# Gated delta rule: the products of a triangular inverse over the whole TensorE array with the 64 changed columns, and norms from one-column products

## The chip, the cores and the metric

The kernel runs on one core of one Trainium2 chip. The metric is the device time of one execution in microseconds; smaller is better. One profiled execution gives the rows that are shown below.

## The reference

Two transformer-like blocks work on a sequence of 1024 tokens of width 1024, in float32. The change touches only the gated delta rule, one of the mixers of the first block: four heads of 128, computed in chunks. For each chunk and head a unit lower triangular system is solved, and q and k are normalised beforehand:

```python
def l2norm(x):
    return x * lax.rsqrt(jnp.sum(x * x, axis=-1, keepdims=True) + EPS)

def gated_delta_rule_chunked(q, k, v, g, beta):
    ...
    L = jnp.where(strict, jnp.einsum('nbhid,nbhjd->nbhij', kb, kc) * decay, 0.0)
    rhs = jnp.concatenate([vc * bc[..., None], kb * jnp.exp(gc)[..., None]], axis=-1)
    sol = lax.linalg.triangular_solve(eye + L, rhs, left_side=True, lower=True, unit_diagonal=True)
    u = sol[..., :Dv]
    w = sol[..., Dv:]
    ...
    def step(S, inp):
        v_new = u_i - jnp.einsum('bhcd,bhde->bhce', w_i, S)
        ...
```

Around it stand a conformer convolution (31 taps along time, `cfm_dw_w`), projections, an output projection, then cross attention, a feed-forward layer, and a second block of two further linear-attention mixers. None of these is changed.

## The kernel before, in words

All of the work is put on the engines in an order that a scheduler fixes when the program is built; each engine then goes through its own queue in that order and waits where data is not there.

The first stage works on two halves of 512 tokens. Dense projections are done by `mm3` (lines 178 to 180): three matmuls with 128 weight columns and 512 (or 256, 264) moving columns each, because weights and inputs are split into a high and a low part. The gated delta rule is the generator `gdn`, called four times: for the halves 0 and 1 and for the head pairs 0 and 1. `weave` runs it against a second generator with dense work (projections, the convolution of the conformer in `s1_conv`, its norm, the output projection), so that steps of both alternate. The calls take place at about 87 to 204, 237 to 364, 355 to 499 and 507 to 621 us of the profiled execution.

One call of `gdn` first sums the squares of q and k over d (lines 538 to 546): ACT squares four tiles of 128 x 512, each goes as the moving operand through a product with a block of 32 columns of ones (L541), the four results lie in four groups of 32 partitions, ACT copies them (L543), and four transposes (L546) turn them so that the token is the partition.

Then four chunks of 128 tokens follow, two chains of two, staggered by `LAG` steps. Each chunk inverts a 128 x 128 triangle per head (two heads together), made of two diagonal halves of 64 (`lo`, `hi`) and the block between them. Inside the halves it doubles the size of the inverted blocks in five levels. A level does the product `U` by `Xm` (L611), a copy to `Q` on ACT (L614), the product `Y` by `Q` (L617), two predicated copies on DVE into `Xm`, one for each half (L620), two transposes of `Xm` (L623) and a copy to `Y` on ACT (L625). Each product is done as four matmuls of 64 x 64 weights and 64 moving columns: two heads by two halves, each half in its own quadrant of the array. After the levels two more products give the block between the halves (L629, L634), with two matmuls of 64 x 64 each.

A float32 matmul stands in the trace as two records, and so does its weight load; a product of four matmuls is therefore `x8`.

DVE, besides the small steps of `gdn`, does the 31 taps of the conformer convolution (L480, 240 instructions of 128 x 512), which the scheduler is told to put at low priority; they lie between the predicated copies. POOL and ACT split the weights that come from HBM.

Of the kernel before, what the change touches and what calls it, by code (L numbers as in the profile page):

```python
# [9 lines left out]
F32 = mybir.dt.float32  # L10
F32R = mybir.dt.float32r
I32 = mybir.dt.int32
U8 = mybir.dt.uint8
AF = mybir.ActivationFunctionType
ALU = mybir.AluOpType
AX = mybir.AxisListType

P = 128
T = 1024
# [42 lines left out]
def weave(main, f, rate):  # L62
    """`rate` steps of f after each of main, then the rest of f"""
    due = 0.0
    for _ in main:
        due += rate
        while due >= 1:
            due -= 1
            next(f, None)
    run(f)  # L70


class Net:
# [72 lines left out]
    # weights: src [pairs of k tiles, 128, 2, columns]  # L146
# [14 lines left out]
    def wplan(self, specs):  # L161
        """the units that wpair() hands out, in order"""
# [3 lines left out]
    def wpair(self):  # L166
        """the next two k tiles, with the loads and splits of the following pairs under way"""
# [14 lines left out]
    # out[c, t]: 4 column tiles of 128, free = t  # L182
# [9 lines left out]
    # out[t, c]: t tiles of 128, free = columns  # L192
# [23 lines left out]
    # rows r [128, 1024] at t tile -> x hi/lo  # L216
# [12 lines left out]
    # rms norm of rows, times g, to x hi/lo  # L229
# [49 lines left out]
    def postnorm(self, y, g, hsrc, hdst):  # L279
        """y: two tiles [P, 4, 512]; y = hsrc + rms(y) g, also to hdst"""  # L280
# [12 lines left out]
    def norm_T(self, y, g, shift=None):  # L293
        """rms-normed rows of y (two panels), transposed"""
# [34 lines left out]
    def s1_open(self):  # L329
# [7 lines left out]
        lf = self.R([P, 6, P])  # L337
        nc.sync.dma_start(lf, a["lvl"])
        self.lvl = p.tile([P, 6, P], U8, name="lvl")
# [12 lines left out]
        nc.vector.tensor_scalar(self.nea, self.nea, -1.0, None, ALU.mult)  # L352
        self.S = []
# [5 lines left out]
    def s1_qkv(self, u, xh, xl, qk, vv, gate):  # L359
        """q, k, v of the heads 2u, 2u + 1 after the short convolution, [d, t], and their gates, rows"""  # L360
# [22 lines left out]
        # the heads 0 and 1 bring the eight logits along  # L383
# [31 lines left out]
    def s1_specs(self):  # L415
        """the weights of stage 1 in the order of their use"""
# [5 lines left out]
    def s1_ab(self, ab):  # L422
        """log decay and beta, [t, chunk, head]"""
# [37 lines left out]
    def s1_conv(self, j, xh, xl, cc):  # L461
        """gated and convolved conformer channels, [c, t]"""
# [52 lines left out]
    def gdn(self, u, qkv, dec, gate):  # L515
        """heads 2u, 2u + 1, 4 chunks of 128; multiplies the normed rows into `gate`"""
# [19 lines left out]
        # squares of q and k, summed over d  # L536
        pr = self.M()
        for j in range(4):
            sq = p1.tile([P, HT], F32, name="cv", tag="cv", bufs=2)
            nc.scalar.activation(sq, qk[:, j, :], AF.Square)  # L540
            mm(pr[32 * j : 32 * j + 32, :], lhsT=self.ones[:, 0:32], rhs=sq, start=True, stop=True)  # L541
        sq = p1.tile([P, HT], F32, name="cv", tag="cv", bufs=2)
        nc.scalar.copy(sq, pr)  # L543
        pn = self.M([P, 4, 4, 32])
        for c in range(NTT):
            tr(pn[:, c, :, :], sq[:, c * P : (c + 1) * P], self.ident)  # L546
        sk, qn, kn, bb, be, so = (p1.tile([P, 8], F32, name="gn", tag="gn", bufs=10) for _ in range(6))
        v.tensor_scalar(c42(sk), pn[:, :, 2:4, 0], EPS, None, ALU.add)
        v.tensor_scalar(c42(qn), pn[:, :, 0:2, 0], EPS, 128.0 * EPS, ALU.add, ALU.mult)
# [5 lines left out]
        def chunk(c):  # L555
# [19 lines left out]
            # decays  # L575
# [10 lines left out]
            # scores  # L586
# [8 lines left out]
            # (I + L)^-1 by doubling; U = -L^T, Xm the inverse within blocks, Y its transpose  # L595
            lv = lambda b: self.lvl[:, b, :].unsqueeze(1).to_broadcast([P, 2, P])
            Y = tl("Y", 2)
            nc.gpsimd.tensor_copy(Y, self.ident.unsqueeze(1).to_broadcast([P, 2, P]))
            v.copy_predicated(Y, lv(0), U)
# [6 lines left out]
            lo, hi = slice(0, 64), slice(64, P)  # L606
            for b in range(1, 6):
                pm = self.M([P, 8, 64], ns)
                for j in range(2):
                    for r in (lo, hi):  # L610
                        mm(pm[r, j, :], lhsT=U[:, j, r], rhs=Xm[:, j, r], start=True, stop=True)  # L611
# [3 lines left out]
                for j in range(2):  # L615
                    for r in (lo, hi):
# [848 lines left out]
```

## Time and profile before

| | |
|---|---|
| time, median of 3 runs | 3004.94 us (3001.94 to 3011.28) |
| span of the profiled execution | 3007.8 us |
| PE busy | 2823.5 us (94%) |
| DVE busy | 1813.9 us (60%) |
| ACT busy | 1135.2 us (38%) |
| POOL busy | 1234.5 us (41%) |
| gated delta rule and what is woven with it | about 86 to 622 us of the span |

The span runs from the first to the last instruction of the profiled execution; no time of that execution outside the span is given. Matmul records overlap, since they are pipelined: a busy share of PE says whether anything was in the array, and the pace is read from the starts of successive records.

### The profile page before, as it was taken

The numbers are of one execution on the slowest core, as the hardware profiler recorded it, in microseconds if no ns is written. First come the engines' busy times: TensorE is split into PE (matmuls) and PEld (weight loads), VectorE is DVE, ScalarE is ACT, GpSimd is POOL, SyncE is SP. The second block draws the span as 40 slices with busy tenths as digits, with TensorE's granted clock in tenths as the row PEclk, the third lists the DMA queues.
The fourth block names the chain that finished last, engine by engine and source line by source line (L and its number), as shares of the span: only waits on it lengthen the run. The fifth ranks groups of instructions, "written<-read, shape, count | busy, mean of one in ns | idle before, by whom it ended". The sixth has DMA issues, their size and how long they took to land.

```text
span 3007.8 us, 41965 instructions
## 1 busy us (share of the span) xinstructions
PE 2823.5 (94%) x15828; PEld 2232.1 (74%) x15828; DVE 1813.9 (60%) x3605; ACT 1135.2 (38%) x2273; POOL 1234.5 (41%) x913
## 2 busy tenths in 40 slices
PE   7999898998999999899899999999999999999998
PEld 6676676777877777677677777787777777777776
DVE  6698889866345765743855556737545366464444
ACT  4443534455444433233433333232233333232333
POOL 3333323333342554354454544343443543434443
PEclk9999999999999999999999999999999999999999
DMA  4112111146242633622422225121323332222222
GB/s 152 50 64 64 50 45 55 36 133 192 68 140 86 202 99 100 208 91 84 130 91 91 85 91 170 51 88 56 96 74 97 99 119 71 82 63 83 85 75 101
DMA packets 136715, 287.07 MB, mean 95 GB/s; under 512 B 9792, under 2 KB 12736, under 8 KB 136512
## 3 DMA queue, kind: packets, MB, share of 16 engines
q1 hardware_dynamic: 136512, 284.38, 29.3%
q8 instruction: 125, 2.05, 0.3%
q14 instruction: 78, 0.64, 0.1%
HBM read 265.99 MB, written 18.35 MB: 95 GB/s over the span
## 4 chain that ended last, share of the span: by engine, by line
PE 49%; DVE 14%; ACT 2%; issue 2%; DMA 2%; POOL 1%; SPq 0%; ACTq 0%; DVEq 0%; POOLq 0%
PE pa L178 15%; PE pa L179 14%; PE pa L180 14%; DVE fo L824 3%; PE pm L944 2%; DVE fo L822 1%; POOL wlo L144 1%; DMA wad<-in_w_ada 1%; DVE fo L829 1%; DVE fh L819 1%; DVE pad L818 1%; DVE gl L144 1%; PE pm L1001 0%; PE pm L990 0%; PE pm L1000 0%
## 5 line engine op out<-in xcount | busy, mean ns | idle before, releaser
L144 POOL TENSOR_TENSOR wlo<-raw,whi 128x512 fp32r<-128x512 f32 (+1 forms) x792 | 1137.7, 1442 | 1668.7 <-ACT whi L143 1590.6
L143 ACT CAST whi<-raw 128x512 fp32r<-128x512 f32 (+1 forms) x808 | 496.7, 620 | 1131.3 <-PE pa L180 603.8
L178 PE MATMUL pa<-x,whi 128*128 128x512 f32 x1376 | 567.4, 413 | 18.8 <-ACT x L1130 10.3
L178 PE MATMUL pa<-whi,x 128*128 128x512 f32 (+2 forms) x1408 | 555.3, 396 | 12.4 <-ACT z L1015 3.8
L180 PE MATMUL pa<-x,wlo 128*128 128x512 f32 x1376 | 552.1, 401 | 0.1
L179 PE MATMUL pa<-x,whi 128*128 128x512 f32 x1376 | 551.9, 401 | 0.0
L180 PE MATMUL pa<-whi,x 128*128 128x512 f32 (+2 forms) x1408 | 547.5, 389 | 0.0
L179 PE MATMUL pa<-wlo,x 128*128 128x512 f32 (+2 forms) x1408 | 546.4, 388 | 0.0
L178 PEld LDWEIGHTS pa<-x,whi 128*128 128x128 f32 x1376 | 261.7, 190 | 82.1 <-ACT x L1130 11.2
L178 PEld LDWEIGHTS pa<-whi,x 128*128 128x128 f32 x1408 | 265.5, 189 | 75.6 <-issue 6.3
L180 PEld LDWEIGHTS pa<-x,wlo 128*128 128x128 f32 x1376 | 261.7, 190 | 62.5 <-issue 2.7
L180 PEld LDWEIGHTS pa<-whi,x 128*128 128x128 f32 x1408 | 265.5, 189 | 54.0 <-issue 0.9
L179 PEld LDWEIGHTS pa<-wlo,x 128*128 128x128 f32 x1408 | 265.6, 189 | 52.4 <-issue 1.2
L179 PEld LDWEIGHTS pa<-x,whi 128*128 128x128 f32 x1376 | 262.1, 190 | 54.2 <-issue 3.4
L480 DVE SCALAR_TENSOR_TENSOR e<-padc,cw,e 128x512 f32<-128x512 f32 x240 | 197.3, 852 | 1.2
L824 DVE SCALAR_TENSOR_TENSOR fo<-pad,cols,fo 128x512 f32<-128x512 f32 x176 | 168.5, 985 | 0.7
L178 PE MATMUL pa<-whi,e 128*128 128x512 f32 x352 | 143.3, 407 | 25.8 <-DVE e L847 20.4
L819 DVE COPY fh<-pad 128x2 f32<-128x2 f32 x88 | 27.3, 310 | 196.4 <-ACT pad L817 196.4
L179 PE MATMUL pa<-wlo,e 128*128 128x512 f32 x352 | 142.2, 404 | 0.0
L180 PE MATMUL pa<-whi,gl 128*128 128x512 f32 x352 | 141.9, 403 | 0.0
L144 DVE TENSOR_TENSOR x<-pm,x 128x512 fp32r<-128x512 f32 x112 | 75.0, 685 | 67.8 <-ACT x L143 67.3
L178 PEld LDWEIGHTS pa<-whi,e 128*128 128x128 f32 x352 | 68.0, 193 | 46.7 <-DVE e L847 23.9
(354 smaller groups left out, 3848.7 us busy)
## 6 DMA issues: line engine op xcount, KB each, us to landing
raw<-in_w_in SPq DMA_DIRECT2D x112, 512.0 KB, 3.7
raw<-in_ffn_w_up SPq DMA_DIRECT2D x88, 512.0 KB, 3.8
raw<-in_ffn_w_down SPq DMA_DIRECT2D x44, 512.0 KB, 4.0
raw<-in_w_out SPq DMA_DIRECT2D x32, 512.0 KB, 3.9
raw<-in_w_qf SPq DMA_DIRECT2D x32, 512.0 KB, 3.7
h<-e SPq DMA_DIRECT2D x48, 256.0 KB, 3.0
r<-h SPq DMA_DIRECT2D x24, 512.0 KB, 4.5
wad<-in_w_ada SPq DMA_DIRECT2D x24, 512.0 KB, 4.4
```

The source lines that it names most:

```text
L143: self.nc.scalar.copy(hi, src)
L144: (lo_eng or self.nc.vector).tensor_tensor(lo, src, hi.bitcast(F32), ALU.subtract)
L178: mm(ps, lhsT=lh, rhs=rh, start=first, stop=False)
L179: mm(ps, lhsT=lh, rhs=rl, start=False, stop=False)
L180: mm(ps, lhsT=ll, rhs=rh, start=False, stop=last)
L480: v.scalar_tensor_tensor(o, pad[:, k : k + HT], w(k), o, ALU.mult, ALU.add)
L818: v.tensor_copy(pad[:, :2], fh[:, i, :])
L819: v.tensor_copy(fh[:, i, :], pad[:, HT:])
L822: v.tensor_scalar(o, pad[:, 2:], self.col(k0 + 2), self.col(FB0 + i), ALU.mult, ALU.add)
L824: v.scalar_tensor_tensor(o, pad[:, k : k + HT], self.col(k0 + k), o, ALU.mult, ALU.add)
L829: v.tensor_tensor(ua, ua, ub, ALU.mult)
L944: mm(pm[64 * e : 64 * e + 64, c, :], lhsT=kG[:, s], rhs=q[:, s], start=True, stop=True)
```

## The change

The two diagonal halves are no longer multiplied in quadrants. Since `U` and `Y` hold both halves in one 128 x 128 tile, one matmul per head over the whole array does both. A level changes only the columns of `Xm` whose bit of that level is 0, which are 64 of the 128, so these columns alone are the moving operand (`left`, a strided view), and one predicated copy over 128 partitions puts the result back; its mask is laid out for those 64 columns. The block between the halves is done over the whole array too, with a `Qz` whose other columns stay zero. For the norms, the squared tile becomes the weights, and one column of ones the moving operand: 16 products that give the sums with the token as the partition at once, so that the copy and the four transposes fall away.

```diff
-        lf = self.R([P, 6, P])
+        lf = self.R([P, P + 320])
...
+        self.Qz = []
+        for n in range(2):
+            z = p.tile([P, 2, P], F32, name=f"Qz{n}")
+            nc.gpsimd.memset(z, 0.0)
+            self.Qz.append(z)
...
-        pr = self.M()
+        pn = self.M([P, 4, 4])
         for j in range(4):
             sq = p1.tile([P, HT], F32, name="cv", tag="cv", bufs=2)
             nc.scalar.activation(sq, qk[:, j, :], AF.Square)
-            mm(pr[32 * j : 32 * j + 32, :], lhsT=self.ones[:, 0:32], rhs=sq, start=True, stop=True)
-        sq = p1.tile([P, HT], F32, name="cv", tag="cv", bufs=2)
-        nc.scalar.copy(sq, pr)
-        pn = self.M([P, 4, 4, 32])
-        for c in range(NTT):
-            tr(pn[:, c, :, :], sq[:, c * P : (c + 1) * P], self.ident)
+            for c in range(NTT):
+                mm(pn[:, c, j : j + 1], lhsT=sq[:, c * P : (c + 1) * P], rhs=self.ones[:, 0:1], start=True, stop=True)
...
             for b in range(1, 6):
-                pm = self.M([P, 8, 64], ns)
+                n, w = 64 >> b, 1 << b
+                left = Xm.rearrange("p h (n s w) -> p h n s w", s=2, w=w)[:, :, :, 0, :]
+                pm = self.M([P, 4, 64], ns)
                 for j in range(2):
-                    for r in (lo, hi):
-                        mm(pm[r, j, :], lhsT=U[:, j, r], rhs=Xm[:, j, r], start=True, stop=True)
+                    mm(pm[:, j, :], lhsT=U[:, j, :], rhs=left[:, j, :, :], start=True, stop=True)
                 yield
                 Q = tl("Q")[:, :, 0:64]
                 nc.scalar.copy(Q, pm[:, 0:2, :])
                 for j in range(2):
-                    for r in (lo, hi):
-                        mm(pm[r, 2 + j, :], lhsT=Y[:, j, r], rhs=Q[:, j, :], start=True, stop=True)
+                    mm(pm[:, 2 + j, :], lhsT=Y[:, j, :], rhs=Q[:, j, :], start=True, stop=True)
                 yield
-                for r in (lo, hi):
-                    v.copy_predicated(Xm[r, :, r], lv(b)[r, :, r], pm[r, 2:4, :])
+                mask = self.lvl[:, P + 64 * (b - 1) : P + 64 * b].rearrange("p (n w) -> p n w", w=w)
+                v.copy_predicated(left, mask.unsqueeze(1).to_broadcast([P, 2, n, w]),
+                                  pm[:, 2:4, :].rearrange("p h (n w) -> p h n w", w=w))
...
             pm = self.M([P, 4, 64], ns)
             for j in range(2):
-                mm(pm[hi, j, :], lhsT=U[lo, j, hi], rhs=Xm[lo, j, lo], start=True, stop=True)
+                mm(pm[:, j, :], lhsT=U[:, j, :], rhs=Xm[:, j, lo], start=True, stop=True)
             yield
-            Q = tl("Q")
-            nc.scalar.copy(Q[hi, :, lo], pm[hi, 0:2, :])
+            Q = self.Qz[ns]
+            nc.scalar.copy(Q[:, :, lo], pm[:, 0:2, :])
             for j in range(2):
-                mm(pm[lo, 2 + j, :], lhsT=Q[hi, j, lo], rhs=Y[hi, j, hi], start=True, stop=True)
+                mm(pm[:, 2 + j, :], lhsT=Q[:, j, :], rhs=Y[:, j, hi], start=True, stop=True)
```

The scheduler also moves instructions. In PE's queue the first levels of the first call of `gdn` stand as follows before; L178 to L180 are the dense matmuls, L602 and L623 transposes, L611 and L617 the two products of a level.

```order
L611 MATMUL pm<-Xm,U 64x64 x4
L602 MATMUL pm<-ident,Y 128x128 x2
L180 MATMUL pa<-x_126,wlo 128x512
L178 MATMUL pa<-x_126,whi 128x512
L617 MATMUL pm<-Q,Y 64x64 x4
L611 MATMUL pm<-Xm,U 64x64 x4
L179 MATMUL pa<-x_127,whi 128x512
L180 MATMUL pa<-x_126,wlo 128x512
L623 MATMUL pm<-ident,Xm 128x128 x2
L617 MATMUL pm<-Q,Y 64x64 x4
```

At the same place the changed program has (L613 and L618 are the products, L625 the transposes of `Xm`):

```order
L613 MATMUL pm<-Xm,U 128x64 x2
L179 MATMUL pa<-x_131,whi 128x512
L180 MATMUL pa<-x_130,wlo 128x512
L618 MATMUL pm<-Q,Y 128x64 x2
L602 MATMUL pm<-ident,Y 128x128 x2
L178 MATMUL pa<-x_130,whi 128x512
L625 MATMUL pm<-ident,Xm 128x128 x2
L179 MATMUL pa<-x_131,whi 128x512
L613 MATMUL pm<-Xm,U 128x64 x2
L180 MATMUL pa<-x_130,wlo 128x512
```

The products have half as many matmuls and still lie between dense matmuls; their places among these shift by one or two.

In PE's queue the norms of the first call read, before and then in the changed program (L541 and L547 are the products with ones, L546 the transposes):

```order
L541 MATMUL pm<-cv,ones 32x512
L180 MATMUL pa<-x_126,wlo 128x512
L178 MATMUL pa<-x_126,whi 128x512
L541 MATMUL pm<-cv,ones 32x512
L179 MATMUL pa<-x_127,whi 128x512
L180 MATMUL pa<-x_126,wlo 128x512
L178 MATMUL pa<-x_126,whi 128x512
L179 MATMUL pa<-x_127,whi 128x512
L546 MATMUL pm<-ident,cv 128x128 x4
```

```order
L547 MATMUL pm<-ones,cv 128x1 x8
L179 MATMUL pa<-x_131,whi 128x512
L180 MATMUL pa<-x_130,wlo 128x512
L178 MATMUL pa<-x_130,whi 128x512
L547 MATMUL pm<-ones,cv 128x1 x4
```

Eight or four one-column products now stand where one or two products of 512 columns stood, and nothing follows the last of them before DVE reads the sums.

In DVE's queue, late in the levels of the second call of `gdn`, the predicated copies (L620, now L621) stand between taps of the convolution (L480, now L485), before and then in the changed program:

```order
L620 COPY_PREDICATED Xm<-lvl,pm 64x2x64 x4
L480 SCALAR_TENSOR_TENSOR e_746<-padc,cw,e_746 128x512 x4
L620 COPY_PREDICATED Xm<-lvl,pm 64x2x64 x4
L480 SCALAR_TENSOR_TENSOR e_746<-padc,cw,e_746 128x512 x3
L620 COPY_PREDICATED Xm<-lvl,pm 64x2x64 x2
```

```order
L621 COPY_PREDICATED Xm<-lvl,pm 128x8x16
L485 SCALAR_TENSOR_TENSOR e_755<-padc,cw,e_755 128x512 x3
L621 COPY_PREDICATED Xm<-lvl,pm 128x8x16
L621 COPY_PREDICATED Xm<-lvl,pm 128x4x32
L485 SCALAR_TENSOR_TENSOR e_755<-padc,cw,e_755 128x512 x3
```

One copy of 128 partitions stands for two of 64, behind about as many taps as before.

## Rows read from the trace of the kernel before

**Rows 1.** The page: busy time by engine, then PE's clock in 40 slices.

```profile
PE 2823.5 (94%) x15828; PEld 2232.1 (74%) x15828; DVE 1813.9 (60%) x3605; ACT 1135.2 (38%) x2273; POOL 1234.5 (41%) x913
PEclk9999999999999999999999999999999999999999
```

**Rows 2.** Busy time by stretch, us: length, engines, clock, DMA share, GB/s.

```profile
86.00:400.00 314.00, 291.06 (x2139) 216.75 (x2140) 252.07 (x576) 141.63 (x330) 101.88 (x82) 0.99 0.17 55
400.00:580.00 180.00, 165.46 (x1161) 126.08 (x1160) 173.84 (x342) 76.65 (x185) 60.55 (x46) 0.97 0.16 50
580.00:622.00 42.00, 42.00 (x351) 31.68 (x352) 25.67 (x75) 24.88 (x68) 7.89 (x8) 1.00 0.09 26
```

**Rows 3.** Timeline, a lone level product between dense matmuls: start, duration, instruction.

```profile
306.94 0.40 PE L179 MATMUL pm<-x,whi 128*128 128x512 f32 x1
307.27 0.45 PE L617 MATMUL pm<-Q,Y 128*64 128x64 f32 x8
307.65 0.50 PE L180 MATMUL pm<-x,wlo 128*128 128x512 f32 x1
307.99 0.39 PE L178 MATMUL pm<-x,whi 128*128 128x512 f32 x1
308.21 0.40 PE L179 MATMUL pm<-x,whi 128*128 128x512 f32 x1
```

**Rows 4.** Timeline, two level products behind each other between dense matmuls.

```profile
314.31 0.28 PE L180 MATMUL pa<-whi,x 128*128 128x264 f32 x1
314.52 0.74 PE L611 MATMUL pm<-Xm,U 128*64 128x64 f32 x16
...
315.41 0.28 PE L179 MATMUL pa<-wlo,x 128*128 128x264 f32 x1
```

**Rows 5.** Timeline, a product for the block between the halves.

```profile
182.68 0.28 PE L180 MATMUL pa<-whi,x 128*128 128x256 f32 x1
182.89 0.44 PE L629 MATMUL pm<-Xm,U 64*64 64x64 f32 x4
...
183.49 0.28 PE L179 MATMUL pa<-wlo,x 128*128 128x256 f32 x1
```

**Rows 6.** Timeline, float32 matmuls over the whole array: 128, then 16 moving columns.

```profile
308.45 0.38 PE L589 MATMUL pm<-e 128*128 128x128 f32 x2
308.67 0.39 PE L590 MATMUL pm<-e 128*128 128x128 f32 x2
...
354.62 0.30 PEld L448 LDWEIGHTS pm<-glog,tri 128*128 128x128 f32 x2 [1.36 <-DVE glog L439]
354.83 0.30 PEld L449 LDWEIGHTS pm<-glog,ones 128*128 128x128 f32 x2
```

**Rows 7.** Groups of instructions, 86 to 640 us: count, busy us, mean ns, idle before.

```profile
L611 PE MATMUL pm<-Xm,U 128*64 128x64 f32 x640 | 36.5, 233 | 0.0
L620 DVE COPY_PREDICATED Xm<-lvl,pm 64x128 f32<-64x128 uint8 x160 | 47.7, 299 | 36.3 <-PE pm L617 15.6 <-ACT Y L625 9.7 <-ACT whi L143 4.1
L599 DVE COPY_PREDICATED Y<-lvl,U 128x256 f32<-128x256 uint8 x16 | 8.3, 519 | 0.0
```

**Rows 8.** Busy time of the predicated copies L620 alone, 400 to 580 us.

```profile
400.00:580.00 180.00, 12.48 (x42) 0.97 0.16 50
```

**Rows 9.** Timeline, one product with ones, then the four transposes of the norms.

```profile
238.32 0.40 PE L179 MATMUL pa<-x,whi 128*128 128x512 f32 x1
238.65 1.05 PE L541 MATMUL pm<-cv,ones 128*32 128x512 f32 x2
...
239.97 0.39 PE L178 MATMUL pa<-x,whi 128*128 128x512 f32 x1
...
242.31 0.60 PE L546 MATMUL pm<-ident,cv 128*128 128x128 f32 x4
```

**Rows 10.** Waits, 86 to 640 us: total, times, longest.

```profile
PE pm L623 <- DVE Xm L620: 6.2, 12, 1.3
PE pm L568 <- DVE Vs L574: 4.1, 3, 2.3
```

More of the change, by code (lines that the diff above doesn't have):

```diff
@@ L336, in s1_open @@
         self.trineg = ld("trineg", [P, P])
-        lf = self.R([P, 6, P])
+        lf = self.R([P, P + 320])
         nc.sync.dma_start(lf, a["lvl"])
-        self.lvl = p.tile([P, 6, P], U8, name="lvl")
+        self.lvl = p.tile([P, P + 320], U8, name="lvl")
         nc.gpsimd.tensor_copy(self.lvl, lf)
@@ L540, in gdn @@
             nc.scalar.activation(sq, qk[:, j, :], AF.Square)
-            mm(pr[32 * j : 32 * j + 32, :], lhsT=self.ones[:, 0:32], rhs=sq, start=True, stop=True)
-        sq = p1.tile([P, HT], F32, name="cv", tag="cv", bufs=2)
-        nc.scalar.copy(sq, pr)
-        pn = self.M([P, 4, 4, 32])
-        for c in range(NTT):
-            tr(pn[:, c, :, :], sq[:, c * P : (c + 1) * P], self.ident)
+            for c in range(NTT):
+                mm(pn[:, c, j : j + 1], lhsT=sq[:, c * P : (c + 1) * P], rhs=self.ones[:, 0:1], start=True, stop=True)
         sk, qn, kn, bb, be, so = (p1.tile([P, 8], F32, name="gn", tag="gn", bufs=10) for _ in range(6))
-        v.tensor_scalar(c42(sk), pn[:, :, 2:4, 0], EPS, None, ALU.add)
-        v.tensor_scalar(c42(qn), pn[:, :, 0:2, 0], EPS, 128.0 * EPS, ALU.add, ALU.mult)
+        v.tensor_scalar(c42(sk), pn[:, :, 2:4], EPS, None, ALU.add)
+        v.tensor_scalar(c42(qn), pn[:, :, 0:2], EPS, 128.0 * EPS, ALU.add, ALU.mult)
         ri = self.rsqrt(sk, 8, "g")
@@ L594, in chunk @@
             v.tensor_tensor(At, pk[:, 2:4, :], dd, ALU.mult)
-            lv = lambda b: self.lvl[:, b, :].unsqueeze(1).to_broadcast([P, 2, P])
             Y = tl("Y", 2)
             nc.gpsimd.tensor_copy(Y, self.ident.unsqueeze(1).to_broadcast([P, 2, P]))
-            v.copy_predicated(Y, lv(0), U)
+            v.copy_predicated(Y, self.lvl[:, 0:P].unsqueeze(1).to_broadcast([P, 2, P]), U)
             pm = self.M([P, 4, P], ns)
@@ L1431, in _host @@
                        & ((i[None, :] // b) % 2 == 1))
-    r["lvl"] = np.concatenate([lv[:, :1], lv[:, 1:6].transpose(2, 1, 0)], axis=1)
+    low = [lv[:, l].T.reshape(P, -1, 2, 1 << l)[:, :, 0, :].reshape(P, 64) for l in range(1, 6)]
+    r["lvl"] = np.concatenate([lv[:, 0]] + low, axis=1)
     r["hmask"] = np.tile(np.concatenate([lv[:64, :6, :64], np.eye(64, dtype=f)[:, None, :]], axis=1), (2, 1, 1))
```

## The prediction

> **What bounds the kernel now.** I first read the page [rows 1]: PE is busy for 94% of the span, no other engine for more than 60%, and the clock granted to PE is nine tenths or more of its upper level (2.4 GHz) in every slice. Then the busy times of the stretch in which the gated delta rule runs, cut into three [rows 2]. PE is busy there for 498.5 of 536 us (291.06 + 165.46 + 42.00), so 37.5 us are left in which nothing is in the array. DVE is the second to watch: 252 of 314 us before 400, but 173.84 of 180 between 400 and 580, which is 97%. So PE is the engine whose queue must get shorter, and in the middle stretch DVE's too.
>
> A busy share does not say what one product costs, so I read the timeline around single ones. Between dense matmuls of 512 columns, which follow each other every 0.23 us or a little less (307.99 to 308.21), a lone level product stands at 307.27 [rows 3]. The dense one ahead starts at 306.94, the dense ones behind at 307.65 and 307.99. The reader is to see two things. The product starts 0.33 us after its predecessor, not 0.23: 0.10 us pass with nothing started. And the dense matmul that follows starts with its record, but its successor comes only 0.34 us later: its weights had not been loaded ahead. From 306.94 to 307.99 there are 1.05 us, of which the two dense matmuls would take 0.46, so the product costs the queue **0.59 us**.
>
> When two products stand behind each other [rows 4], the way from 314.31 to 315.41 is 1.10 us; two matmuls of 264 columns take 0.24 of it (0.23 x 264 / 512 each, an estimate), so the pair costs 0.86. The second product adds 0.27. The difference, 0.32 us per stretch, is therefore the price of going into the quadrants and out again, and 0.27 that of a product itself. A product for the block between the halves [rows 5], with half the matmuls, costs 0.81 - 0.23 = 0.58, nearly the same.
>
> The Trainium skill, TensorEngine Tiling, Key Properties, says that a change of tiling mode drains TensorE. The trace agrees: 0.10 us of nothing ahead of the product in the row above.
>
> **The change, part by part.**
>
> *Products.* Four calls of four chunks make 16 chunks; five levels of two products and two more make 12 per chunk, 192 in all; 160 are level products (L611 has 640 records, 8 for each of 80 [rows 7]). In PE's timeline they form 178 stretches, of which 24 hold two products and 154 one or a part of one. Before: 154 x 0.59 + 24 x 0.86 = 111.5 us of PE's queue.
>
> After, a product is two matmuls over the whole array, four records. No row shows 64 moving columns with float32 over the whole array, but two rows stand on either side [rows 6]. With 128 columns two records start every 0.22 us, 0.11 each; with 16 columns the weight loads of two records start 0.21 us apart, 0.105 each. The pace hardly depends on the columns, so it is that of the loads, and 64 columns lie between: I take 0.11, so 0.44 per product (0.42 by the other end). The mode is that of the dense matmuls around it, so I add no price for going in or out. After: 192 x 0.44 = 84.5 us. **Saved: 27 us.** One thing is not bounded by this: the first product of a level (80 of 192) now reads its moving columns from a strided view, and every row of a moving operand here is contiguous. Streaming 64 columns takes at most 0.055 us (half of the 0.11), behind a load of 0.11, so at twice the price it still hides, and I take nothing. If load and stream did not overlap there at all, it would be 4 x 0.055 x 80 = 17.6 us.
>
> *Predicated copies.* Before, two per level, 160, of 0.299 us mean for 64 x 128; over 128 partitions and 256 elements (L599) one takes 0.519 [rows 7]. Since DVE's time goes with the elements of a partition, one copy over 128 partitions and 128 elements should take 0.30: 80 x 0.30 = 24 us less on DVE. If the strided view doubled it, DVE would save nothing. Most of these 24 us are covered by PE. Between 400 and 580, where DVE is full, 42 of the 160 copies lie [rows 8]: there DVE gives 21 x 0.30 = 6.3 us, while PE would give 27 x 42 / 160 = 7.1; I take off 1 us. Elsewhere the shorter copy brings the transposes behind it (L623) nearer: PE waited 6.2 us for them in 12 places [rows 10]. I count 2 of these.
>
> *Norms.* One stretch with ones costs 1.65 - 0.46 = 1.19 us of PE's queue (238.32 to 239.97), the four transposes 4 x 0.11 = 0.44 [rows 9]. Three calls have three such stretches and the fourth two: 3 x (3.57 + 0.44) + 2.38 + 0.44 = 14.8 us. After, 16 products of two records per call at the pace of the loads, 16 x 0.22 = 3.5, in four calls 14.1. So PE gains 0.7 us. A copy on ACT and the transposes also leave the way to the first chunk; the wait of PE for `Vs` (L568), which needs the norms, was 4.1 us [rows 10]. I count 2.
>
> *Small things.* The memsets of `Qz` are ahead of the first stage; POOL then waits for the mask anyway. Uncovered they would be 1 us, at L599's price for the same size. `Qz` is a tile of its own, so its copy no longer waits for readers of `Q`. Nothing taken.
>
> *Friction.* PE's part shrinks, the replies of ACT and DVE between two products do not, and the scheduler shifts the places by one or two dense matmuls. 7% of the stretch is idle now; I take 3 us, a tenth of the gain, back as new waits.
>
> Sum: 27 - 1 + 2 + 0.7 + 2 - 3 = **27.7 us** off the span of 3007.8, which makes 2980. What lies around that span is not given; the median of the runs is 2.9 us below it, so I forecast **2977 us** for the median. What follows 622 us is unchanged.
>
> **The rivals.**
>
> *DVE or the replies hold the chain.* For it: 97% of DVE between 400 and 580, and taps of the convolution still ahead of each copy in its queue. Against it: PE's busy time is as high in the other stretches, where DVE has room. If the middle stretch gave nothing, 118 of 160 parts stay, 27 x 118 / 160 = 20; with the friction doubled, 14 us: 2991. Chance 0.17.
>
> *The strided view is dear.* 27.7 - 17.6 = 10 us gained: 2995. Nothing for or against in the rows. Chance 0.05.
>
> *The drains do not come back: slower.* The Trainium skill, TensorEngine Tiling, When to Use Tiling, recommends row tiling for contractions of 64 or less, which this change gives up. The trace agrees with its half of the matter: a product in quadrants costs 0.27, over the whole array 0.44. Where PE would have waited for ACT or DVE at that place anyhow, the 0.32 us are no loss now, and the change costs 0.17 us per product, 33 us if it were so everywhere. It decides from a share of 27 / (0.32 x 178) = 0.47 of the stretches; at six tenths the span grows by 7 us, to about 3012 in the median. Against it: L611 has no idle time ahead of it at all [rows 7], and the known waits are few [rows 10]. Chance 0.05.
>
> *More than forecast.* If both waits of rows 10 vanish (10.3 us, not 4) and the friction does not come, 27 + 0.7 + 10.3 = 38: 2967. Chance 0.10.
>
> *No effect.* Product costs and waits trade off, within 9 us of now: 0.03.
>
> **How the numbers follow.** The forecast keeps 0.60; its own range is 2969 to 2986 (friction from none to three times, waits from 0 to 8). To leave out no more than 2 in 10 the range takes in the larger gain and the first two rivals: 2963 to 2996. A measurement of this kernel can tell about 0.3%, 9 us, from no change. Faster: 0.60 + 0.17 + 0.10 + most of the 0.05 of the strided view, 0.91. The same: 0.04; slower: 0.05.
>
> **What would show it.** Right: the products appear with four records, 0.44 us from the dense matmul ahead to the one behind beyond their own time; the dense matmul behind has its weights loaded ahead; the copies number 80 at about 0.30 us; norms with 128 records at 0.11; the last product of `gdn` ends some 28 us earlier, and the rest of the span is the same length. Wrong in the pace: first products of a level take 0.6 us or more. Wrong in the bound: idle time of PE in 86 to 600 us grows well beyond 37.5 us, ended by DVE's copies or ACT's `Q` and `Y`. Wrong in the norms: DVE's first read of the sums is not earlier against the last square.

## The result, and the profile after

The changed kernel takes 2988.12 us in the median (2984.09 to 2997.37, five runs) against 3004.94 before (3001.94 to 3011.28). The ratio is 0.9948, 95% interval 0.9929 to 0.9967: some 16 us faster, 10 to 21 by the interval. I had forecast 2977, a gain of 27.7; the time lies in the range of 2963 to 2996 and outside the likeliest case's own range.

The page after answers to [rows 1]: busy time by engine, then PE's granted clock.

```profile
PE 2818.7 (94%) x15268; PEld 2284.3 (76%) x15268; DVE 1785.0 (60%) x3525; ACT 1126.6 (38%) x2264; POOL 1231.9 (41%) x915
PEclk9999999999999999999999999999999999999999
```

DVE has 80 instructions less (3525 against 3605): the second copy of each level is gone. In the windows of [rows 2] after the change (length, busy PE, PEld, DVE, ACT, POOL, clock, DMA):

```profile
86.00:400.00 314.00, 296.57 (x1864) 257.02 (x1864) 244.81 (x542) 139.16 (x337) 100.13 (x84) 0.97 0.18 56
400.00:580.00 180.00, 169.40 (x1070) 144.82 (x1068) 168.38 (x342) 81.66 (x205) 60.38 (x48) 0.97 0.17 50
```

How far the delta rule has come is seen in one pair of rows. In PE's timeline the last product for its output (L664 before, L667 after) and the first product of its norms:

```profile
87.17 1.05 PE L541 MATMUL pm<-cv,ones 128*32 128x512 f32 x4
...
619.24 0.39 PE L664 MATMUL pm<-Q,At 128*128 128x128 f32 x2
```

and after:

```profile
86.27 0.92 PE L547 MATMUL pm<-ones,cv 128*128 128x1 f32 x7
...
598.08 0.39 PE L667 MATMUL pm<-Q,At 128*128 128x128 f32 x2
```

The stretch took 532 us (619.24 - 87.17) and takes 512 (598.08 - 86.27): 20 us less, three quarters of what I had forecast. I call this **the stretch** below. The code behind it was not changed, yet the profiled span is only 12.2 us shorter (2995.6 against 3007.8), because the part behind the stretch is 9 us longer (2397 against 2388). Two things are seen there. PE stood at the lower level of its clock (1.2 GHz) for 102 us of it, 88 before; this profiled execution was the slowest of the five. And the scheduler had put 11 dense matmuls of 512 columns there that lay in the stretch before (934 start in the stretch, 945 before). At 0.23 us each these are 2.5 of the 20 us, an estimate: that work was moved and not saved. With half of the 14 us at the lower clock it makes up the 9. So the length of the stretch, read in one trace, and the ratio of the times stand side by side below.

A level product after the change, the answer to [rows 3]: start and duration in PE's queue, with ACT's copy that waits for it.

```profile
302.40 0.28 PE L179 MATMUL pa<-wlo,x 128*128 128x264 f32 x1
302.52 0.55 PE L613 MATMUL pm<-Xm,U 128*128 128x64 f32 x4
302.89 0.49 PE L180 MATMUL pa<-whi,x 128*128 128x264 f32 x2
303.12 0.27 ACT L616 COPY Q<-pm 128x128 f32<-128x128 f32 x1 [0.29 <-PE pm L613]
303.21 0.28 PE L178 MATMUL pa<-whi,x 128*128 128x264 f32 x1
```

From 302.40 to 303.21 there are 0.81 us; the three dense matmuls of 264 columns take 0.12 each (the spacing of the first two rows), so the product costs PE's queue 0.45 us. I had taken 0.44. The groups of the stretch, answering to [rows 7] and [rows 9] (count, busy us, mean ns, idle before):

```profile
L618 PE MATMUL pm<-Q,Y 128*128 128x64 f32 x320 | 46.1, 268 | 0.0
L613 PE MATMUL pm<-Xm,U 128*128 128x64 f32 x320 | 45.1, 266 | 0.0
L547 PE MATMUL pm<-ones,cv 128*128 128x1 f32 x128 | 18.4, 270 | 0.0
L621 DVE COPY_PREDICATED Xm<-lvl,pm 128x128 f32<-128x128 uint8 x80 | 25.6, 322 | 39.1 <-PE pm L618 35.9 <-ACT Qz L635 2.1 <-ACT Y L627 0.4
```

L613 reads the strided view and L618 does not: 266 and 268 ns. The view costs PE nothing. One copy takes 0.322 us where I had 0.30.

So a lone product and the copies are as forecast and the sum is not. What a product does to those who wait for it is in the next two fences. Before, one level from the first product to the copies, in the timeline:

```profile
543.01 0.45 PE L611 MATMUL pm<-Xm,U 128*64 128x64 f32 x8
...
543.56 0.27 ACT L614 COPY Q<-pm 128x128 f32<-128x128 f32 x1 [0.85 <-PE pm L611]
...
544.05 0.45 PE L617 MATMUL pm<-Q,Y 128*64 128x64 f32 x8
544.61 0.83 DVE L620 COPY_PREDICATED Xm<-lvl,pm 64x128 f32<-64x128 uint8 x3 [0.33 <-PE pm L617]
```

and after:

```profile
113.17 0.55 PE L613 MATMUL pm<-Xm,U 128*128 128x64 f32 x4
...
113.81 0.27 ACT L616 COPY Q<-pm 128x128 f32<-128x128 f32 x1 [0.41 <-PE pm L613]
...
114.30 0.55 PE L618 MATMUL pm<-Q,Y 128*128 128x64 f32 x4
...
114.94 0.30 DVE L621 COPY_PREDICATED Xm<-lvl,pm 128x128 f32<-128x128 uint8 x1 [0.38 <-PE pm L618]
```

From a product's first record to the start of the copy that waits for it, 0.55 and 0.56 us pass before, 0.64 and 0.64 after. Elsewhere the difference is up to 0.15 (144.00 to 144.49 before, 0.49). Over all copies of the stretch that stood waiting for their product at full clock, the medians are 0.53 us on ACT (58 copies) and 0.57 on DVE (18) before, 0.65 (57) and 0.70 (31) after. So over the whole array a product holds PE's queue for less time and answers some 0.12 us later. Two products a level make some 0.25 us more, and the one copy gives back 0.28 (two of 0.30 against one of 0.32). The chain through the copies, which the next level's first product needs, is about as long as before: that is an estimate from these rows, and the experiments test it.

The Trainium skill, TensorE: Matmul & The Clock Gate, Part 2 (Step-by-step), says that the next matmul enters while the previous one's results are still on their way through the array. The trace agrees: 0.45 us of queue, 0.64 to the copy. What the queue gets back and what a waiter gets back are two prices.

### The profile page after: what moved, and what is told of

It is laid out like the page before. It is cut to its first block, busy times and chain, and to the rows that moved or that the text cites. A ratio compares the mean times of both kernels' runs of the same rounds, so it can differ in the third digit from the quotient of the medians.

```text
span 2995.6 us, 40696 instructions
## 1 busy us (share of the span) xinstructions
PE 2818.7 (94%) x15268; PEld 2284.3 (76%) x15268; DVE 1785.0 (60%) x3525; ACT 1126.6 (38%) x2264; POOL 1231.9 (41%) x915
## 4 chain that ended last, share of the span: by engine, by line
PE 60%; DVE 26%; DMA 5%; ACT 4%; issue 4%; POOL 1%; SPq 0%; ACTq 0%; DVEq 0%; POOLq 0%
PE pa L178 16%; PE pa L179 16%; PE pa L180 16%; DVE e L485 3%; DVE fo L827 3%; PE pm L947 2%; DMA wad<-in_w_ada 1%; DVE fo L825 1%; DVE tn L129 1%; ACT junk L227 1%; POOL wlo L144 1%; DVE e L289 1%; PE pm L618 1%; ACT whi L143 1%; PE pm L613 1%
## 5 line engine op out<-in xcount | busy, mean ns | idle before, releaser
L178 PE MATMUL pa<-x,whi 128*128 128x512 f32 x1376 | 571.0, 415 | 20.3 <-ACT x L1133 9.8
L178 PE MATMUL pa<-whi,x 128*128 128x512 f32 (+2 forms) x1408 | 554.8, 395 | 13.9 <-DVE rt L1047 3.9
L180 PE MATMUL pa<-x,wlo 128*128 128x512 f32 x1376 | 553.5, 402 | 0.0
L180 PE MATMUL pa<-whi,x 128*128 128x512 f32 (+2 forms) x1408 | 546.4, 388 | 0.0
L178 PEld LDWEIGHTS pa<-whi,x 128*128 128x128 f32 x1408 | 265.4, 188 | 76.2 <-issue 6.8
L178 PEld LDWEIGHTS pa<-x,whi 128*128 128x128 f32 x1376 | 263.6, 192 | 77.9 <-ACT x L1133 10.6
L180 PEld LDWEIGHTS pa<-x,wlo 128*128 128x128 f32 x1376 | 263.3, 191 | 60.6 <-issue 1.0
L180 PEld LDWEIGHTS pa<-whi,x 128*128 128x128 f32 x1408 | 265.4, 189 | 53.2 <-issue 0.9
L485 DVE SCALAR_TENSOR_TENSOR e<-padc,cw,e 128x512 f32<-128x512 f32 x240 | 201.7, 877 | 0.1
L178 PE MATMUL pa<-whi,e 128*128 128x512 f32 x352 | 145.1, 412 | 27.0 <-DVE e L850 21.3
L180 PE MATMUL pa<-whi,gl 128*128 128x512 f32 x352 | 143.1, 407 | 0.0
L178 PEld LDWEIGHTS pa<-whi,e 128*128 128x128 f32 x352 | 68.8, 195 | 47.9 <-DVE e L850 24.7
```

The costliest lines, as they stand in the source:

```text
L178: mm(ps, lhsT=lh, rhs=rh, start=first, stop=False)
L180: mm(ps, lhsT=ll, rhs=rh, start=False, stop=last)
L485: v.scalar_tensor_tensor(o, pad[:, k : k + HT], w(k), o, ALU.mult, ALU.add)
```

## The experiments

Every kernel was run in five rounds beside the kernel before on the same chip, and the ratio is to that (medians of before from 3004.9 to 3012.1, so the medians of two lines are not to be compared directly). P stands for the whole-array products, C for the single copy per level, N for the new norms. The stretch is read in each kernel's trace, one execution each. So are the last two columns: how long PE stood at the lower level of its clock in the stretch, and how many dense matmuls of 512 columns start in it.

| kernel | what it has | median us | ratio, 95% interval | stretch us | lower clock, us | dense |
|---|---|---|---|---|---|---|
| before | | | 1 | 532 | 17.1 | 945 |
| changed | P, C, N | 2988.12 | 0.9948 [0.9929, 0.9967] | 512 | 30.7 | 934 |
| e1 | P, C | 2988.42 | 0.9942 [0.9926, 0.9959] | 514 | 20.5 | 938 |
| e2 | N | 3016.36 | 1.0031 [1.0020, 1.0041] | 543 | 54.6 | 950 |
| e3 | P, C, N with 128 columns | 2996.13 | 0.9959 [0.9948, 0.9971] | 522 | 34.1 | 938 |
| e4 | P, N | 3007.77 | 0.9998 [0.9989, 1.0007] | 537 | 44.4 | 963 |
| e5 | P | 3009.33 | 0.9991 [0.9981, 1.0000] | 532 | 13.7 | 958 |
| e6 | C (in quadrants) | 3001.84 | 0.9966 [0.9954, 0.9978] | 526 | 23.9 | 938 |
| e7 | before, fewer taps | 3007.50 | 0.9987 [0.9978, 0.9996] | 531 | 23.9 | 938 |
| e8 | changed, fewer taps | 2998.75 | 0.9955 [0.9938, 0.9971] | 519 | 47.8 | 934 |
| e9 | e1, spare copies on DVE | 2996.58 | 0.9961 [0.9947, 0.9976] | 519 | 23.9 | 930 |
| e10 | e1, other rates | 2987.52 | 0.9933 [0.9915, 0.9952] | 513 | 20.5 | 926 |
| e11 | e1, DVE's copy by head | 2995.74 | 0.9958 [0.9942, 0.9974] | 520 | 27.3 | 941 |
| e12 | e1, ACT's copy by head | 2993.39 | 0.9960 [0.9946, 0.9974] | 519 | 23.9 | 938 |

**The parts apart: e1, e2, e4, e5, e6.** e1 is the changed kernel with the norms of before (lines 538 to 549 of the kernel before put back).

> Products over the whole array and the single copies, but the norms as before (32-column blocks of ones, copy, four transposes). Theory A: the forecast of PE's queue was right and what is missing was lost to TensorE's clock. In the changed kernel's trace the granted clock falls to its lower level (1.2 GHz) right behind the one-column products, at 87.8 us for 10.2, at 347.2 for 3.4 and at 497.4 for 10.2 us; before, the stretch up to 622 us had 17.0 us at that level, after it 30.6. Half of the 13.6 us more is 6.8 us. A expects no fall at 88 and 347 us, and a median some 5 to 8 us below that of the changed kernel: 2980 to 2983. Theory B: DVE and the replies between products hold the chain, and the norms do nothing: 2986 to 2990, as the changed kernel.

The levels alone have the whole gain: 0.9942 against 0.9948. Theory A does not hold in the time, although its premise does: without the new norms PE stood at the lower clock for 10 us less.

e2 is the kernel before with the new norms alone:

```
-            mm(pr[32 * j : 32 * j + 32, :], lhsT=self.ones[:, 0:32], rhs=sq, start=True, stop=True)
...
+            for c in range(NTT):
+                mm(pn[:, c, j : j + 1], lhsT=sq[:, c * P : (c + 1) * P], rhs=self.ones[:, 0:1], start=True, stop=True)
```

> The norms by one-column products alone, levels in quadrants with two copies as before. Theory A: the clock falls behind the one-column products cost more than the queue saves (0.7 us) and the shorter way to the first chunk brings (at most 4.1 us): 2 to 7 us slower than before, with the granted clock at the lower level near 88 us. Theory B: norms are neutral or a little better, 0 to 3 us faster than before.

The new norms make the kernel before slower, 1.0031, 9 us, more than theory A's 2 to 7. That is a loss that I had priced nowhere.

e4 and e5 take the single copy out, with the new and with the old norms:

```
-                v.copy_predicated(left, mask.unsqueeze(1).to_broadcast([P, 2, n, w]),
-                                  pm[:, 2:4, :].rearrange("p h (n w) -> p h n w", w=w))
+                for r in (lo, hi):
+                    v.copy_predicated(left[r], mask[r].unsqueeze(1).to_broadcast([64, 2, n, w]),
+                                      pm[r, 2:4, :].rearrange("p h (n w) -> p h n w", w=w))
```

> The whole change, but each level's predicated copy is done as two of 64 partitions again, so DVE gets back about 80 x 0.30 = 24 us. By the forecast's terms DVE's relief was worth 2 us of waits and the single copies let the middle stretch keep up (6.3 us of DVE there): 2 to 9 us slower than the changed kernel, 2990 to 2997. If DVE does not pace the stretch at all: within 2 us of it, 2986 to 2990. If DVE is the bound throughout (theory B): up to 20 us slower.

e4 gives back the whole gain (0.9998 against 0.9948, 15 us), not the 2 to 9 us of the forecast's terms. Against e2 it is 10 us faster by the ratios: with the new norms in place the products do gain without the single copy. The stretch shows 6 us of that, and PE stood at the lower clock for 10 us less.

> Products over the whole array alone: two predicated copies of 64 partitions per level and the norms as before. Theory A (PE's queue bounds the stretch): the 27 us of PE come off nearly whole, 2980 to 2987. Theory C, from the run with two copies (no faster than before although its products are over the whole array): DVE's queue paces the stretch, in which DVE keeps some 85 us of idle time whatever PE does, so that only DVE's time counts: 3000 to 3008, the same as before or a little better.

e5 bears on the largest term: the products alone give 0.9991, at most 6 us, and the stretch is 532 us as before. It holds 13 dense matmuls more than before, some 3 us, and each of its two copies of a level takes 0.324 us instead of 0.299, because they too go into the strided view. Yet the price of the quadrants is gone: read as in [rows 3], a lone product costs 0.46 us of the queue in the median of 74 places, against 0.59 of 51 before. Part of what was saved came back as idle time of PE. In the two windows it is 45.7 us, 37.5 before and 28.0 in the changed kernel:

```profile
86.00:400.00 314.00, 288.80 (x1772) 237.04 (x1773) 258.42 (x582) 138.23 (x334) 106.69 (x83) 0.99 0.19 56
400.00:580.00 180.00, 159.49 (x973) 132.27 (x971) 174.66 (x337) 74.00 (x177) 59.21 (x46) 0.98 0.16 48
```

In the list of waits of 86 to 640 us (engine, line, releaser: total, times, longest), PE's weight loads for the second product of a level, before:

```profile
PEld pm L617 <- ACT Q L614: 8.2, 29, 0.4
```

and in the kernel with the products alone, with the waits that grew behind them:

```profile
PE pm L630 <- DVE Xm L626: 9.2, 15, 1.6
PEld pm L622 <- ACT Q L620: 6.0, 21, 0.3
```

L630 are the transposes behind the copies. PE waits 9.2 us for them there, 6.2 before [rows 10], and 2.2 in the changed kernel:

```profile
PE pm L625 <- DVE Xm L621: 2.2, 5, 0.7
PEld pm L625 <- DVE Xm L621: 8.3, 20, 1.1
PEld pm L618 <- ACT Q L616: 2.5, 9, 0.3
```

The weight loads of the same transposes wait too: 8.3 us for the copy in the changed kernel, and 14.5 in e5 and 10.7 before for something that the trace does not name. By both queues e5 waits most there and the changed kernel least.

e6 is the other half, the kernel before with one copy of 128 partitions per level. It copies both halves of the columns (256 elements a partition) under the same mask, so that it needs no other layout:

```
-                for r in (lo, hi):
-                    v.copy_predicated(Xm[r, :, r], lv(b)[r, :, r], pm[r, 2:4, :])
+                v.copy_predicated(
+                    Xm.rearrange("p h (s w) -> p h s w", s=2),
+                    self.lvl[:, b, :].rearrange("p (s w) -> p s w", s=2).unsqueeze(1).to_broadcast([P, 2, 2, 64]),
+                    pm[:, 2:4, :].unsqueeze(2).to_broadcast([P, 2, 2, 64]),
+                )
```

> The kernel before with products in quadrants and norms unchanged, but one predicated copy of 128 partitions and 256 elements per level instead of two of 64 partitions and 128 elements. Such a copy takes 0.435 us in the median (the first copy of each chunk, before), two take 0.60, so DVE is relieved of 80 x 0.165 = 13 us and PE of nothing. Theory A: 3003 to 3008, within what its waits for the copies were (6.2 us). Theory C: 9 to 13 us faster, 2992 to 2998.

The copy alone gives 0.9966, 10 us in the times and 6 in the stretch, although each takes 0.441 us here:

```profile
L619 DVE COPY_PREDICATED Xm<-lvl,pm 128x256 f32<-128x256 uint8 x80 | 34.4, 441 | 34.0 <-PE pm L617 15.3 <-ACT Y L628 14.1 <-ACT Xm L605 1.6
```

So in the stretch the parts don't add up: 0 us for the products and 6 for the copy, 18 for both (e5, e6 and e1). Some 5 us of the difference between e5 and e1 are the 20 dense matmuls that only e5 still has there. In the times the parts are 3 and 10 us and both together 17, and the intervals are too wide to tell 17 from 13. That each part is worth more where the other is in place is thus read from single traces. e5 and e6 both fit theory C, in which DVE's queue paces the stretch; the next two test it.

**Is DVE the bound? e7 and e8.** Both leave out 4 of the 31 taps of the convolution, some 26 us of DVE's work in the stretch:

```
-                for k in range(30):
+                for k in range(4, 30):
```

> The kernel before without 4 of the 31 taps of the conformer convolution (32 instructions of 0.82 us, 26 us of DVE; the output lacks these taps). No work of PE changes. Theory A: at most 6 us faster, 2999 to 3008. Theory C: 18 to 26 us faster, 2980 to 2988.

> The changed kernel without the same 4 taps (the output lacks them). If DVE is still what paces the stretch once the copies are single (theory C throughout): 18 to 26 us below the changed kernel, 2963 to 2971. If PE's queue, lengthened by the clock falls, has become the bound there: at most 8 us below it, 2980 to 2988.

0.9987 and 0.9955: 4 us for the kernel before, nothing that can be told for the changed one (0.9948). In e8 PE stood at the lower clock for 17 us more than in the changed kernel; with half of that as lost it could hide a gain of up to 9 us, but not the 18 to 26 of theory C. DVE's busy time between 400 and 580, 173.84 us in [rows 2], is 165.93 in e7:

```profile
400.00:580.00 180.00, 166.02 (x1172) 125.85 (x1170) 165.93 (x334) 78.19 (x191) 58.14 (x46) 0.97 0.15 48
```

PE's is 166.02 there against 165.46. DVE's amount of work does not set the end; that reading of the first rival falls.

**The chain, lengthened without PE: e9, e11, e12.** All three have the products and copies of e1. e9 adds a copy per level that nobody waits for, behind the transposes:

```
+                v.copy_predicated(self.spare, self.lvl[:, P : 2 * P], Xm[:, 0, :])
```

> The products and the single copy of the change with the norms of before, and in each of the 80 level steps one more predicated copy on DVE (128x128 values of one head, by the row of the single copy about 0.3 us), which is issued behind the transposes, goes to a tile that nobody reads, and has nobody waiting for it: some 24 us of DVE work, about what the second copy of a level cost before. What gained in the one copy was a shorter chain of a level (product, copy, product, copy, transposes), not DVE's work. Theory A (the chain): a copy beside the chain costs little, the time lies within 4 us of the kernel without it (ratio to before 0.993 to 0.996). Theory B (DVE's load): the gain of the single copy is given back, 8 to 16 us (ratio 0.997 to 1.000).

e11 cuts the one copy in two that both stand in the chain:

```
-                v.copy_predicated(left, mask.unsqueeze(1).to_broadcast([P, 2, n, w]),
-                                  pm[:, 2:4, :].rearrange("p h (n w) -> p h n w", w=w))
+                for j in (1, 0):
+                    v.copy_predicated(left[:, j, :, :], mask, pm[:, 2 + j, :].rearrange("p (n w) -> p n w", w=w))
```

> The products of the change with the norms of before, and the one copy of a level cut in two that both stand in the chain: all 128 partitions, one head each, the second head first, so that the transposes of the first head, which stand first on TensorE, wait for both. Two copies of half the values should take some 0.2 us each, about 0.1 us longer than the one, in a chain of 80 steps, and 8 us more DVE work. Theory A (the chain's length through the copies decides): 3 to 10 us slower than with one copy (ratio 0.995 to 0.998), TensorE waiting longer for the transposes' copy. Theory B (only the two halves of the partitions, that is the split of the array, made the two copies dear): no more than 2 us slower (ratio 0.993 to 0.995).

e12 cuts ACT's copy of `Q` in the same way:

```
-                nc.scalar.copy(Q, pm[:, 0:2, :])
+                for j in (1, 0):
+                    nc.scalar.copy(Q[:, j, :], pm[:, j, :])
```

> The products and the single copy of the change with the norms of before, and ACT's copy of Q, between the two products of a level, cut into two copies of one head each, the second head first, so that the second product, whose first head stands first, waits for both. By the rows of 128x128 at 0.27 us and 128x256 at 0.37 a copy of 128x64 should take some 0.22 us, the two 0.17 longer than the one: 13.6 us more in the dependent chain of 80 levels, on an engine that is busy for less than half of the stretch, and nothing more on TensorE or DVE. Theory A (the time of the replies in a level decides, whatever the engine's load): 4 to 10 us slower than with one copy (ratio 0.9955 to 0.998). Theory B (only what TensorE and DVE have to do counts): within 2 us of the kernel with one copy (ratio 0.9935 to 0.995).

The groups that were added, in e9 (the spare copy), e11 and e12:

```profile
L632 DVE COPY_PREDICATED spare<-lvl,Xm 128x128 f32<-128x128 uint8 x80 | 28.4, 354 | 0.7
```

```profile
L626 DVE COPY_PREDICATED Xm<-lvl,pm 128x64 f32<-128x64 uint8 x160 | 30.3, 237 | 39.8 <-PE pm L622 23.1 <-ACT Y L631 10.0 <-ACT junk L497 2.6
```

```profile
L621 ACT COPY Q<-pm 128x64 f32<-128x64 f32 x160 | 26.0, 218 | 42.7 <-PE pm L617 42.1
```

e12 adds 0.17 us per level (2 x 0.218 against 0.267) on an engine that is busy for 254.85 of 554 us, and nothing on PE or DVE; the stretch grows by 5 us and the ratio by as much. e11 adds 0.15 us per level and 4.8 us of DVE's time (30.3 against 25.5): the stretch grows by 6. Both fall in the range of the chain's theory. The two chains of a call run side by side, so only 40 of the 80 levels stand one behind another, which the expectations leave out: 0.17 and 0.15 us make 7 and 6 us, an estimate near what was found. It is weak evidence all the same. The intervals of the ratios overlap that of e1, all three kernels are set against this one e1, and in their traces PE stood at the lower clock for 3 to 7 us more than in e1's. e9, which I had as free under that theory, loses too: 5 us of the stretch, 6 by the ratio, for 28.4 us of DVE. The expectation of neither theory fits: a copy beside the chain costs a fifth of its time, where one in the chain costs about what it takes. I take it that DVE runs in order and two chunks are under way, so that a spare copy of one stands ahead of the needed copy of the other; no run tests this. The same could hold for ACT's work in e12, so the chain is the likeliest reading and not shown alone.

**The norms: e3.** The changed kernel with 128 moving columns in the norms' products instead of one, the same count of products:

```
-                mm(pn[:, c, j : j + 1], lhsT=sq[:, c * P : (c + 1) * P], rhs=self.ones[:, 0:1], start=True, stop=True)
+                i = NTT * j + c
+                mm(pn[:, i : i + P], lhsT=sq[:, c * P : (c + 1) * P], rhs=self.ones, start=True, stop=True)
```

> The whole change, but each product with ones has 128 moving columns instead of one (the later products overwrite the columns that are not needed). The pace of the loads, 0.11 us per record, should be the same, so PE's queue has the same length. Theory A: if few moving columns per load are what the clock reacts to, there are no falls behind the norms, and the median is 5 to 8 us below the changed kernel's, 2980 to 2983. Theory B: 2986 to 2990. If the clock falls all the same, it is not the number of moving columns but the waiting around the norms.

It is no faster (0.9959; the stretch 10 us longer), so theory A does not hold in the time. What speaks for the clock is the traces. Busy times and clock of the first 14 us in the changed kernel, then in e3, then the matmuls there in the changed kernel:

```profile
86.00:100.00 14.00, 14.00 (x59) 12.28 (x59) 5.24 (x26) 3.90 (x7) 2.58 (x2) 0.63 0.13 39
86.00:100.00 14.00, 11.53 (x65) 10.18 (x66) 8.38 (x31) 4.97 (x10) 3.87 (x5) 0.88 0.28 76
```

```profile
88.86 0.63 PE L180 MATMUL pa<-x,wlo 128*128 128x512 f32 x1
89.29 0.63 PE L178 MATMUL pa<-x,whi 128*128 128x512 f32 x1
89.71 1.70 PE L547 MATMUL pm<-ones,cv 128*128 128x1 f32 x8
```

The granted clock is 0.63 over the window, that is, its lower level (1.2 GHz) for most of it; ahead of the fall PE ran the one-column products. Dense matmuls are 0.43 us apart (88.86 to 89.29), 0.23 elsewhere [rows 3]. The same 0.63 stands in e2 and e4, and 1.00 in e1 and e5, which have the old norms. With 128 columns it is 0.88, but over its whole stretch e3 has as much time at the lower clock as the changed kernel (34.1 and 30.7 us). In e2 the clock over 86 to 640 us is lowest; the kernel before follows it:

```profile
86.00:640.00 554.00, 522.25 (x3767) 406.43 (x3768) 461.08 (x1005) 242.04 (x588) 166.34 (x137) 0.95 0.16 50
86.00:640.00 554.00, 514.15 (x3714) 386.93 (x3715) 460.68 (x1012) 254.15 (x609) 176.36 (x140) 0.98 0.16 51
```

The 0.03 between is 33 us more at half the clock (554 x 0.03 x 2), and costs up to half of it, 16: enough for the 11 us by which e2's stretch is longer. With both other parts in place the clock is 0.97, and the stretch is not longer than without the new norms (512 and 514). The table shows that the loss goes with the clock: the new norms bring 37.5 us more at the lower level in e2 (against before), 30.7 in e4 (against e5) and 10.2 in the changed kernel (against e1), and the stretch changes by +11, +5 and -2 us. If half of that time is lost, an estimate, the norms apart from the clock gain 8, 10 and 7 us; but the same sum gives no gain for e3 against e1. Why the clock was low for longer where the old copies stand beside the new norms stays open.

**More even cover: e10.** The rates at which other work is put between the steps of the delta rule, changed so that it lasts over all 99 steps of a stretch:

```
-RATE = (0.9, 1.1, 1.2, 0.55)
+RATE = (0.97, 0.97, 1.33, 0.45)
```

> The products and the single copy of the change with the norms of before, and the four rates at which steps of other work are put between the steps of the delta rule changed from 0.9, 1.1, 1.2, 0.55 to 0.97, 0.97, 1.33, 0.45, so that in each of the four stretches the other work is spread over all 99 steps instead of ending early or being left over. Theory A (TensorE waits where a dependent step comes back before its cover is done, and the cover is uneven): up to 6 us faster than without it, ratio 0.992 to 0.994. Theory B (the cover within a stretch is moved by the scheduler anyway): within 3 us of the kernel without it, either way.

0.9933 against 0.9942 of e1, 513 us against 514: no difference that can be told. No kernel here beats the changed one by more than the runs can tell.

## Why the prediction was right in its sign and range and wrong in its sum

*What a product costs.* Right for a lone one: 0.45 us of PE's queue against 0.44 (0.46 in the median of 63 places), four records, no price for the strided view on PE, nothing lost ahead of it. The rival of the dear view is out. Wrong for two behind each other, which I had at 0.88. From 537.49 to 538.93 there are 1.44 us, 0.98 without the two dense matmuls, and seven such places give 0.90 to 0.99; before, 16 places had a median of 0.845:

```profile
537.49 0.48 PE L178 MATMUL pa<-whi,x 128*128 128x512 f32 x1
537.80 1.00 PE L618 MATMUL pm<-Q,Y 128*128 128x64 f32 x8
538.61 0.48 PE L179 MATMUL pa<-wlo,x 128*128 128x512 f32 x1
538.93 0.39 PE L180 MATMUL pa<-whi,x 128*128 128x512 f32 x1
```

With 24 pairs on either side and these medians the products save some 21 us of the queue and not 27, an estimate.

*"Saved: 27 us".* This step failed. It priced only the queue: 178 stretches at 0.59 or 0.86 against 192 at 0.44. Alone (e5) it is worth nothing in the stretch and at most 6 us in the times. Besides the pairs, two things were left out. The answers of a product come later over the whole array, 0.64 us after its start against 0.49 to 0.56, which I could have read in the trace of before for one side and had no row for on the other. At 0.25 us a level, with 40 levels one behind another, that is 10 us, an estimate. And part of what the queue saves is time in which PE then waits: in e5 PE's idle time grows by 8 us, and its waits for DVE's copies from 6.2 to 9.2 us. My rival "the drains do not come back" had the second of these, and stood at 0.05; with two copies the outcome is near its point of no gain and no loss, but no run measures the share of the stretches that it rests on.

*"Most of these 24 us are covered by PE".* Failed too, on the other side. I took the copies for 1 us, 2 of waits less 1 of DVE's limit. Alone they give 6 us of the stretch (e6, with copies of twice the elements), on top of the products 18 (532 to 514, e5 to e1), some 5 of which are dense matmuls that moved behind it. PE's busy share of 93% does not say that the work of another engine is hidden: the second copy stood in the chain that PE's own next transposes wait for.

*"Friction: 3 us, a tenth of the gain".* This is where the two errors meet. The replies of ACT and DVE between two products do not shrink, I wrote; they grew. Of the 27, with two copies nothing is left in the stretch, with one 18.

*The first rival, "DVE or the replies hold the chain".* It gave 2991 and the time is 2988.12, nearer than my forecast. Its half on the replies is what e5, e11 and e12 speak for; its evidence, DVE's 97% between 400 and 580, was wrong: 26 us less work for DVE changes nothing that can be told (e8) or 4 us (e7).

*Norms.* PE's price was right (16 records in the 1.78 us from 230.94 to 232.72). The 2 us of the wait for `Vs` did not come: 3.7 us after, 4.1 before [rows 10]. By my own sign the step was wrong in the first call, where DVE reads the sums 4.73 us behind the last square (4.16 before) while PE is at the lower clock, and right in the other three (3.02, 4.39 and 6.76 us against 4.17, 5.11 and 9.68).

```profile
230.94 1.92 PE L547 MATMUL pm<-ones,cv 128*128 128x1 f32 x16
232.72 0.48 PE L180 MATMUL pa<-x,wlo 128*128 128x512 f32 x1
```

```profile
PE pm L569 <- DVE Vs L575: 3.7, 3, 2.3
```

The clock was not in my sum at all; the norms alone, with what the clock takes there, cost 9 us (e2).

*"Idle time of PE well beyond 37.5 us".* It is not: 17.43 us in 86 to 400 and 10.60 in 400 to 580, by the windows above, against 22.94 and 14.54 in [rows 2]. In e5 it did grow, to 45.7 us, so the sign was a good one for the products and the single copy took it away. It misses what is lost to the clock: between 86 and 100 us PE is busy for all of the 14 us at a clock of 0.63.

## What to carry to other kernels

A product in a dependent chain has two prices: what it takes from the queue, and how long after its start the next engine can begin; read both, the second from a product's first record to the copy that waits for it. When a change makes the queue cheaper and the chain longer, look for the step that shortens the chain as well, and time each part alone and both together, since they need not add up. When a stretch of two traces is compared, count the work that lies in it and look at its clock first. A busy share of 93% on one engine does not hide the other engines' work where this engine's next instruction waits for it.

## What was not expected of the hardware

- Products over the whole array occupied PE for less time than the same work in quadrants between dense matmuls (0.45 us against 0.59 for a lone one; two behind each other took more, 0.98 against 0.845), but the waiting copy began later (0.64 us after the start against 0.49 to 0.56).
- Streams of one-column products, put in alone, went with a lower granted clock around them (0.63 in the first 14 us, 0.95 over 86 to 640 us) and made the kernel 0.3% slower.
- The two copies of 64 partitions take 0.324 us each into the strided view (e5), 0.299 into the contiguous one [rows 7]:

```profile
L626 DVE COPY_PREDICATED Xm<-lvl,pm 64x128 f32<-64x128 uint8 x160 | 51.7, 324 | 36.7 <-PE pm L622 21.2 <-ACT Y L632 5.0 <-ACT junk L497 3.7
```
